# Recurrent stage of a decoder layer: new counted delays, and three groups of matmuls in other places of the order

## The chip, the cores and the metric

The kernel runs on one core of one Trainium2 chip. A core has a matrix engine (PE, whose weight loads are the row PEld), a vector engine (DVE), a scalar engine (ACT), a general engine (POOL) and a queue that issues transfers (SP). They work side by side and wait for each other through semaphores. Each works through its own instructions in the order in which they were issued. The metric is the time of one execution in microseconds (us), as the device measures it.

## The reference, cut to what matters

One layer of a decoder on 1024 tokens of width 1024. The first sub-layer joins a recurrent branch and an attention branch, each weighted by a sigmoid gate; then come a cross-attention into 256 memory tokens and a gated convolutional MLP. The change lies in the recurrent branch (8 heads of 64). What it computes, per token:

```python
w_log = -softplus(-(w0 + tanh(wl) @ w2)) - 0.5
decay = exp(-exp(w_log))
a = sigmoid(a0 + al @ a2)
kk = k * k_k
kk = kk / max(sqrt(sum(kk * kk, axis=-1)), 1e-12)     # per head
k = k * (1.0 + (a - 1.0) * k_a)
erase, refill = -kk, kk * a
def step(state, inp):
    r_t, w_t, k_t, v_t, a_t, b_t = inp
    sa = einsum('bhvk,bhk->bhv', state, a_t)
    state = state * w_t + sa * b_t + v_t * k_t
    return state, einsum('bhvk,bhk->bhv', state, r_t)
_, y = lax.scan(step, state0, (r, decay, k, v, erase, refill))
y = (y - mean(y)) * rsqrt(var(y) + GN_EPS) * gn_g + gn_b
mixed = (g_a * (y_a @ merge_p_a) + g_b * (y_b @ merge_p_b)) @ mix_w_o
```

## The kernel before, in words

Large products are made in float32 as three passes (`mm3`, lines 196 to 198: high times high, high times low, low times high) over 512 columns. Such a group of three matmuls is called a **triple** below.

The recurrent stage works on **8 units**: four head pairs, each in two halves of 512 tokens, each half in 8 chunks of 64 tokens. For every unit there are five generators, each of which issues a few instructions and then yields:

- `operands(i)`: the decay products (`pw`, `pa`, lines 583 and 585), the scan over the logarithms (`CU`), the exponentials; the square of the key (`TMP`, line 601, on ACT) and its sums per head (`vs`, line 549, on PE), the way back (`bc`, line 564), the scaled keys, and the product `gl` (line 632). From `gl` comes the triangular matrix `LT`, of which 16 by 16 blocks go through DRAM (`d1`), are inverted on DVE by substitution (`stmp` and `DB`, lines 654 and 655), and come back through DRAM (`d2`) as `DD` and `EE` (line 667, 16 transfers issued by SP).
- `couplings(i)`: `gb`, `gk`, then three transposes of four blocks each (`tr`, line 707: of `BB`, `KB_` and the values `Xv`), whose results ACT copies out (`KS`, line 721) or DVE copies out after taking the mean away (`ZV` and `SV`, line 719, eight instructions behind one reduction, line 711), and the bonus product `pbo` (line 728), copied out by DVE (`BV`, line 729).
- `inverse(i)`: five small products (`q`, `d`, `e`, `q`, `e`) that finish the inverse from its blocks.
- `recurrence(i)`: for each chunk three products one after another: `x` (line 783), `sa` (788), `z` (794). Each needs what DVE or ACT copied out of the one before.
- `outputs(i)`: `psy`, the group norm (another `vs` and `bc`), the store to `ya`.

The order on PE alone is written out by the program when it is built: a loop keeps a **counted clock**. A generator yields two numbers: how long the work just issued counts on PE, and how long after that its next step comes due. At every turn the loop takes the first class with a due step, in the order of the line below, so that dense work fills what the recurrences leave:

```python
classes = (recurrences, outputs_, inverses, couplings_, operands_, dense, [wide])
```

`dense` are the input projections of this branch (`prj`), `wide` the products of the merge gates (`gt`); each step of both is one triple and counts 0.69. All 256 gate triples are needed later. Those that the recurrent stage did not take are issued between and inside the blocks of the attention stage behind it, by `fill`, at a fixed number per block; after the gates `fill` goes on with the merge products (`mg`), and what is left of those runs in one piece behind the attention blocks. An inverse comes due `L_SUBST = 36` counted us after its `gl`. The other engines' orders come from the scheduler of the language.

PSUM banks go round: the products named `pw`, `pa`, `vs`, `bc`, `gl`, `gb`, `gk`, `tr` and `pbo` take three banks in turn, so that each waits until the result three places ahead of it was copied out.

Of the kernel before, what the change touches and what calls it, by code (L numbers as in the profile page):

```python
# [126 lines left out]
def layer_kernel(ctx: ExitStack, tc, I, out, cst):  # L127
# [42 lines left out]
    def pss(name="pss"):  # L170
        return bank("s", name)
# [322 lines left out]
    def e2(name):  # L494
        return rp.tile([P, HALF], F32, tag="e", name=name, bufs=9)
# [79 lines left out]
    def operands(me):  # L575
# [3 lines left out]
        lo = LO[:, half * HALF:(half + 1) * HALF]  # L579
        cs_ = slice(hp * P, hp * P + P)  # L580

        ps = pss("pw")
        PE.matmul(ps, lw[0:64, cs_], lo[0:64], start=True, stop=True)
        ps2 = pss("pa")
# [7 lines left out]
        S.activation(E2, CU, AF.Exp, scale=DEC)  # L592
        G.tensor_tensor(E3, CU, E3, op=OP.subtract)
        S.activation(E3, E3, AF.Exp, scale=-DEC)
        yield 1.3, 0.5
        while not projections[3 * hp].done:
            yield 0, 0.5
        Xk = Xs[hp, 1][half]

        TMP, KKN = e2("TMP"), e2("KKN")  # L600
        S.activation(TMP, Xk, AF.Square, scale=pc("rwkv_k_k", hp))
        w = norm_sums(TMP, pss, ew, 64.0, None)
        yield 1.0, 4.5
        while not projections[3 * hp + 1].done:
            yield 0, 0.5
        Xr = Xs[hp, 0][half]
# [64 lines left out]
    def couplings(me):  # L671

        u, (hp, half) = units[me], divmod(me, 2)
        Xr, E3, ET, BH, KH, BB, KB_, TMP = u.operands
        Xv = Xs[hp, 2][half]
        AMR = k8("AMR")
        for h, rw in enumerate(rows_h):
            V.tensor_tensor(AMR[rw, :, 1, h, :], r8(Xr[rw]), r8(ET[rw]), op=OP.mult)
            S.activation(AMR[rw, :, 0, h, :], r8(E3[rw]), AF.Copy)

        GB, KS, SV, ZV = k2("GB"), k4("KS"), k4("SV"), k4("ZV")
        u.AMR, u.GB, u.KS, u.SV, u.ZV = AMR, GB, KS, SV, ZV
        if half == 0:
            for h, rw in enumerate(rows_h):
                G.memset(ZV[rw, 0, h, :], 0.0)
        yield 0, 3.0
        ps = pss("gb").rearrange("p (c t) -> p c t", t=CH)
        for c in range(NC8):
            for h, rw in enumerate(rows_h):
                PE.matmul(ps[rw, c], BH[rw, c * CH:(c + 1) * CH], AMR[rw, c, 1, h, :], start=True, stop=True)  # L690
        V.tensor_tensor(GB, ps, bc(gmask[:, CH:P], NC8), op=OP.mult)
        for j in range(2):
            ps = pss("gk").rearrange("p (c a t) -> p c a t", a=2, t=CH)
            for ci in range(4):
                c = 4 * j + ci
                for h, rw in enumerate(rows_h):
                    PE.matmul(ps[rows_h[1 - h], ci], KH[rw, c * CH:(c + 1) * CH], AMR[rw, c, :, h, :], start=True, stop=True)
            for h in range(2):
                rx = rows_h[1 - h]
                m = gmask[rx].rearrange("p (a t) -> p a t", a=2)[:, None].to_broadcast([64, 4, 2, CH])  # L700
                V.tensor_tensor(AMR[rx, 4 * j:4 * j + 4, :, h, :], ps[rx], m, op=OP.mult)
        yield 2.9, 1.0

        for src, flip, dsts in ((BB, 0, (KS,)), (KB_, 1, (KS,)), (Xv, 1, (ZV, SV))):
            ps = pss("tr").rearrange("p (c n) -> p c n", n=P)
            for c in range(4):
                PE.transpose(ps[:, c, :], src[:, c * P:(c + 1) * P], ident)
            if src is Xv:

                mv = sm.tile([P, 4, 2], F32, name="vm", tag="vm", bufs=2)  # L710
                V.tensor_reduce(mv, ps.rearrange("p c (h d) -> p c h d", h=2), axis=AX.X, op=OP.add)
            for q, rq in enumerate(rows_h):
                for h in range(2):
                    ro = rows_h[1 - h] if flip else rows_h[h]
                    for dst in dsts:
                        o, v = dst[ro, q:NC8:2, h, :], ps[rq, :, h * 64:h * 64 + 64]
                        if src is Xv:
                            m = mv[rq, :, h][:, :, None].to_broadcast([64, 4, 64])
                            V.scalar_tensor_tensor(o, m, -1.0 / 64, v, op0=OP.mult, op1=OP.add)
                        else:  # L720
                            S.activation(o, v, AF.Copy)
            yield 0.5, 0.8
        if me >= 2:
            while not outputs_[me - 2].done:
                yield 0, 0.5
        u.BV = ec("BV")
        ps = pss("pbo")
        PE.matmul(ps, ones, TMP, start=True, stop=True)
        V.scalar_tensor_tensor(u.BV, ps, 64.0, Xv, op0=OP.mult, op1=OP.mult)
        yield 1.1, 0  # L730

    def inverse(i):
# [5 lines left out]
            for rw in rows_h:  # L738
                PE.matmul(ps[rw, c, :], UU[rw, c], DD[rw, c], start=True, stop=True)
        S.activation(QQ, ps, AF.Copy)  # L740
        yield 0.8, 1.2
        ps = bank("b", "d1").rearrange("p (c d) -> p c d", d=CH)
        for c in range(NC8):
            for h in range(2):
# [2 lines left out]
        for h in range(2):  # L747
            a = slice(h * 64, h * 64 + 32)
            V.tensor_tensor(DD[a, :, 0:32], DD[a, :, 0:32], ps[a, :, 0:32], op=OP.add)
        yield 0.5, 1.2  # L750
        ps = bank("b", "e1").rearrange("p (c d) -> p c d", d=CH)
        for c in range(NC8):
            for h, rw in enumerate(rows_h):
                PE.matmul(ps[rw, c, :], QQ[rw, c], EE[rw, c, h], start=True, stop=True)
        for h, rw in enumerate(rows_h):
            V.tensor_tensor(EE[rw, :, h], EE[rw, :, h], ps[rw], op=OP.add)
        yield 0.8, 0.8
        ps = bank("b", "q2").rearrange("p (c d) -> p c d", d=CH)
        for c in range(NC8):
            for h in range(2):  # L760
# [2 lines left out]
        for h in range(2):  # L763
            b = slice(h * 64 + 32, h * 64 + 64)
            S.activation(QQ[b, :, 0:32], ps[b, :, 0:32], AF.Copy)
        yield 0.5, 1.0
        ps = bank("b", "e2").rearrange("p (c d) -> p c d", d=CH)
        for c in range(NC8):
            for h in range(2):
# [8 lines left out]
    def recurrence(i):  # L778
        u, (hp, half) = units[i], divmod(i, 2)
        AMR, EE, KS, SV, ZV, WC = u.AMR, u.EE, u.KS, u.SV, u.ZV, u.WC  # L780
        for c in range(NC8):
# [1 line left out]
            PE.matmul(ps[:, 0:P], pair(AMR[:, c, 0]), pair(ZV[:, c]), start=True, stop=True)  # L783
            XS = sm.tile([P, P], F32, name="XS", tag="XS", bufs=2)
            V.tensor_copy(XS, ps[:, 0:P])
            yield 0.3, 1.1
            ps = bank("c", "sa")
            PE.matmul(ps[:, 0:P], pair(EE[:, c]), XS, start=True, stop=True)
            V.tensor_copy(SV[0:64, c, 0, :], ps[0:64, 0:64])
            S.activation(SV[64:128, c, 1, :], ps[64:128, 64:128], AF.Copy)  # L790
            yield 0.3, 1.3
            if not (half == 1 and c == NC8 - 1):
                ps = bank("c", "z")
                PE.matmul(ps[:, 0:P], pair(KS[:, c]), pair(SV[:, c]), start=True, stop=True)
# [2 lines left out]
                for h, rw in enumerate(rows_h):  # L797
                    dst = ZV[rw, c + 1, h, :] if c < NC8 - 1 else units[i + 1].ZV[rw, 0, h, :]
                    V.scalar_tensor_tensor(dst, ZV[rw, c, h, :], WC[rw, c, :], ps[rw, h * 64:h * 64 + 64], op0=OP.mult, op1=OP.add)
                yield 0.3, 1.7  # L800

    def outputs(i):
        u, (hp, half) = units[i], divmod(i, 2)
# [12 lines left out]
        S.activation(Y, psy, AF.Copy)  # L816
        Y2 = ey("Y2")
        S.activation(Y2, Y, AF.Square)
        yield 2.8, 2.5
        w = norm_sums(Y2, pso, ew, 1.0, epsgn)  # L820
        yield 1.0, 4.0
        ps = norm_back(w, pso)
# [45 lines left out]

    def may_project(hp, j):
        if hp == 0:  # L870
            return first.done
        return couplings_[2 * hp - 1].done if j == 2 else couplings_[2 * hp - 2].done and hasattr(units[2 * hp - 1], "WC")

    def gates_timed():
# [2 lines left out]

    first = Task(decays())
    projections = [Task(projected(hp, j), (lambda hp=hp, j=j: may_project(hp, j))) for hp in range(4) for j in (1, 0, 2)]
    operands_ = [Task(operands(i), (lambda i=i: first.done if i == 0 else couplings_[i - 1].done)) for i in range(8)]  # L880
    couplings_ = [Task(couplings(i), (lambda i=i: hasattr(units[i], "WC") and projections[i // 2 * 3 + 2].done and (i < 2 or hasattr(units[i - 2], "out")))) for i in range(8)]
    inverses = [Task(inverse(i), (lambda i=i: clock[0] >= getattr(units[i], "due", 1e9)), True) for i in range(8)]
    recurrences = [Task(recurrence(i), (lambda i=i: inverses[i].done and couplings_[i].done), True) for i in range(8)]
    outputs_ = [Task(outputs(i), (lambda i=i: recurrences[i].done)) for i in range(8)]
    wide = Task(gates_timed())
    dense = (first, *projections)
    classes = (recurrences, outputs_, inverses, couplings_, operands_, dense, [wide])
    with tc.manual_schedule(engines={mybir.EngineType.PE}):
        while not all(t.done for t in outputs_):
# [583 lines left out]
```

## Time and profile before

| | us |
|---|---|
| median of 3 runs | 2306.57 (2303.36 to 2312.32) |
| the profiled execution | 2305.22 |
| its span, first to last instruction | 2303.4 |
| recurrent stage, about | 213 to 790 of the span |
| attention blocks, about | 840 to 1165 of the span |

The profiled execution took 1.8 us more than its span and stands 1.35 us under the median. In the rows below PE's busy time is that of pipelined matmuls whose ends are modelled. An idle time in brackets stands ahead of an instruction and names what ended it. PEclk is the granted clock of TensorE as a share of full speed (1.00 is 2.4 GHz, 0.50 is 1.2 GHz).

### The profile page before, as it was taken

The page shows a single profiled execution, that of the slowest core. Times are in us where ns is not written, and L with a number is a line of the kernel's source. Part 1 is how long each engine was busy: PE and PEld are TensorE (multiplying, and loading weights), DVE is VectorE, ACT ScalarE, POOL GpSimd, SP SyncE. Part 2 cuts the span into 40 slices and gives each one's busy share as a digit, 9 for nine tenths or more (in the row PEclk, how much of TensorE's full clock was granted, in tenths as well). Part 3 has the DMA queues.
Part 4 walks back from the last instruction along what each step waited for, and adds up shares of the span by engine and source line. Part 5 has one row for each costly group of instructions (what it writes and reads, how often), then busy time and mean ns, then how long its engine had stood idle before and what let it go on. Part 6 is the DMA issues. An engine that isn't in the chain of part 4 may idle for free.

```text
span 2303.4 us, 34187 instructions
## 1 busy us (share of the span) xinstructions
PE 2175.1 (94%) x13508; PEld 1788.7 (78%) x13508; DVE 1256.4 (55%) x2495; ACT 897.4 (39%) x1462; POOL 445.9 (19%) x512
## 2 busy tenths in 40 slices
PE   8989989989899879999999999999999999999998
PEld 7988767777678756766669978898888888888886
DVE  4332566666664278788873834456443434444347
ACT  3332343444343356677751433224231313222232
POOL 1212121221220024444440201021010101001013
PEclk9999989999889989999999999999999999999999
DMA  6344111111112412102134321202111111112112
GB/s 206 111 152 141 37 38 41 39 42 45 35 49 66 118 51 78 56 10 60 51 123 152 115 79 55 92 20 64 46 55 37 55 46 46 51 45 69 46 37 83
DMA packets 197933, 158.07 MB, mean 69 GB/s; under 512 B 49301, under 2 KB 173198, under 8 KB 197774
## 3 DMA queue, kind: packets, MB, share of 16 engines
q1 hardware_dynamic: 186062, 139.11, 20.2%
q10 hardware_dynamic: 11136, 14.68, 1.9%
q0 software_dynamic: 576, 2.10, 0.3%
q8 instruction: 107, 1.75, 0.3%
q14 instruction: 52, 0.43, 0.1%
HBM read 125.86 MB, written 29.98 MB: 68 GB/s over the span
## 4 chain that ended last, share of the span: by engine, by line
PE 77%; DVE 10%; DMA 5%; ACT 3%; issue 3%; POOL 1%; SPq 1%; ACTq 0%; DVEq 0%; POOLq 0%
PE up L198 7%; PE up L196 7%; PE up L197 7%; PE dn L196 4%; PE dn L198 4%; PE dn L197 3%; PE op L196 2%; PE op L198 2%; PE op L197 2%; PE gt L196 2%; PE gt L197 2%; PE gt L198 2%; PE prj L196 2%; PE prj L197 2%; DVE wl L202 2%
## 5 line engine op out<-in xcount | busy, mean ns | idle before, releaser
L202 DVE TENSOR_TENSOR wl<-raw,wh 128x1024 fp32r<-128x1024 f32 (+1 forms) x164 | 204.4, 1247 | 274.5 <-ACT wh L201 269.7
L201 ACT ACTIVATE wh<-raw 128x1024 fp32r<-128x1024 f32 (+1 forms) x164 | 173.0, 1055 | 462.8 <-PE dn L198 143.4
L196 PE MATMUL up<-nTh,wh 128*128 128x512 f32 x704 | 276.6, 393 | 0.0
L197 PE MATMUL up<-nTl,wh 128*128 128x512 f32 x704 | 276.5, 393 | 0.0
L198 PE MATMUL up<-nTh,wl 128*128 128x512 f32 x704 | 276.3, 392 | 0.0
L1398 DVE SCALAR_TENSOR_TENSOR cv<-up,pv,cv 128x511 f32<-128x511 f32 (+1 forms) x176 | 131.6, 748 | 146.7 <-ACT cv L1396 144.7
L1422 POOL TENSOR_TENSOR cv<-cv 128x512 f32<-128x512 f32 x44 | 56.7, 1290 | 631.3 <-DVE cl L1402 413.9
L198 PEld LDWEIGHTS up<-nTh,wl 128*128 128x128 f32 x704 | 132.3, 188 | 29.8
L197 PEld LDWEIGHTS up<-nTl,wh 128*128 128x128 f32 x704 | 132.3, 188 | 29.5
L196 PEld LDWEIGHTS up<-nTh,wh 128*128 128x128 f32 x704 | 132.3, 188 | 29.5
L1044 POOL TENSOR_TENSOR pl<-pe,ph 128x512 fp32r<-128x512 f32 x87 | 113.1, 1305 | 161.1 <-ACT ph L1043 134.7
L196 PE MATMUL dn<-wh,gT 128*128 128x512 f32 x352 | 138.3, 393 | 0.0
L198 PE MATMUL dn<-wh,gT 128*128 128x512 f32 x352 | 137.7, 392 | 0.0
L197 PE MATMUL dn<-wl,gT 128*128 128x512 f32 x352 | 137.0, 390 | 0.0
L196 PE MATMUL gt<-xTh,wh 128*128 128x512 f32 x256 | 114.9, 449 | 8.1 <-ACT gst L472 8.1
L1433 DVE SCALAR_TENSOR_TENSOR acc<-acc,dn 128x512 f32<-128x512 f32 x96 | 65.4, 686 | 95.3 <-PE dn L198 94.7
L1396 ACT ACTIVATE cv<-up,pv 128x512 f32<-128x512 f32 x88 | 68.4, 778 | 117.8 <-PE up L198 117.7
L198 PE MATMUL gt<-xTh,wl 128*128 128x512 f32 x256 | 103.2, 403 | 0.0
L197 PE MATMUL gt<-xTl,wh 128*128 128x512 f32 x256 | 103.1, 403 | 0.0
L196 PE MATMUL np<-wh,xTh 128*128 128x256 f32 (+1 forms) x320 | 92.0, 289 | 2.2 <-ACT wh L201 2.2
L196 PE MATMUL prj<-xTh,wh 128*128 128x512 f32 x208 | 91.9, 442 | 1.6 <-ACT wh L201 1.6
L1043 ACT ACTIVATE ph<-pe 128x512 fp32r<-128x512 f32 (+1 forms) x148 | 89.7, 627 | 6.6 <-POOL macc L1161 4.6
(361 smaller groups left out, 5523.8 us busy)
## 6 DMA issues: line engine op xcount, KB each, us to landing
raw<-in_ffn_w_up_dram SPq DMA_DIRECT2D x88, 256.0 KB
raw<-in_w_in_dram SPq DMA_DIRECT2D x37, 512.0 KB
raw<-in_ffn_w_down_dram SPq DMA_DIRECT2D x22, 512.0 KB
gscr<-gst ACTq DMA_DIRECT2D x32, 256.0 KB
xt<-in_x_dram SPq DMA_DIRECT2D x8, 512.0 KB
rawn<-nst SPq DMA_DIRECT2D x32, 128.0 KB
raw<-in_xa_wk_dram SPq DMA_DIRECT2D x8, 512.0 KB
raw<-in_xa_wv_dram SPq DMA_DIRECT2D x8, 512.0 KB
```

The source lines that it names most:

```text
L196: PE.matmul(o, lh, rh, start=start, stop=False)
L197: PE.matmul(o, lh, rl, start=False, stop=False)
L198: PE.matmul(o, ll, rh, start=False, stop=stop)
L201: S.activation(h, src, AF.Copy)
L202: V.tensor_sub(l, src, h.bitcast(F32))
L1043: S.activation(h, e, AF.Copy)
L1044: in_turn("l", LTURN)(l, e, h.bitcast(F32), op=OP.subtract)
L1396: S.activation(c, ps, AF.Identity, scale=pc("cw2", ci), bias=pc("ffn_conv_b", ci))
L1398: V.scalar_tensor_tensor(c[:, s:], ps[:, :HALF - s], pc(nme, ci), c[:, s:], op0=OP.mult, op1=OP.add)
L1422: G.tensor_tensor(c[0], c[0], c[1], op=OP.mult)
L1433: V.scalar_tensor_tensor(v, v, 1.0 if f else ALPHA, ps, op0=OP.mult, op1=OP.add)
```

## The change

It does four things, all in the recurrent stage.

1. In `operands` the square of the key and its sums stand ahead of the decay products, and the first unit's keys are projected ahead of the decay's own inputs (`dense`, `may_project`, `operands_`).
2. In `couplings` the values are transposed first, then `BB` and `KB_`.
3. The counted delays have other values: most in `inverse` are longer, those of `recurrence` are shorter.
4. Nothing is computed otherwise; the number of instructions on PE is the same.

```diff
@@ operands
+        while not projections[3 * hp].done:
+            yield 0, 0.5
+        Xk = Xs[hp, 1][half]
+        TMP, KKN = e2("TMP"), e2("KKN")
+        S.activation(TMP, Xk, AF.Square, scale=pc("rwkv_k_k", hp))
+        yield 0, 1.2
+        w = norm_sums(TMP, pss, ew, 64.0, None)
+        yield 1.0, 0.3
+        while not first.done:
+            yield 0, 0.5
         ps = pss("pw")
         PE.matmul(ps, lw[0:64, cs_], lo[0:64], start=True, stop=True)
...
         S.activation(E3, E3, AF.Exp, scale=-DEC)
-        yield 1.3, 0.5
-        while not projections[3 * hp].done:
-            yield 0, 0.5
-        Xk = Xs[hp, 1][half]
-
-        TMP, KKN = e2("TMP"), e2("KKN")
-        S.activation(TMP, Xk, AF.Square, scale=pc("rwkv_k_k", hp))
-        w = norm_sums(TMP, pss, ew, 64.0, None)
-        yield 1.0, 4.5
+        yield 1.3, 5.0
@@ couplings
-        for src, flip, dsts in ((BB, 0, (KS,)), (KB_, 1, (KS,)), (Xv, 1, (ZV, SV))):
+        for src, flip, dsts in ((Xv, 1, (ZV, SV)), (BB, 0, (KS,)), (KB_, 1, (KS,))):
@@ inverse, behind q, d, e and q
-        yield 0.8, 1.2
+        yield 1.1, 1.2
-        yield 0.5, 1.2
+        yield 0.7, 1.3
-        yield 0.8, 0.8
+        yield 1.1, 1.9
-        yield 0.5, 1.0
+        yield 0.7, 1.1
@@ recurrence, behind x, sa and z
-            yield 0.3, 1.1
+            yield 0.35, 0.8
-            yield 0.3, 1.3
+            yield 0.25, 1.0
-                yield 0.3, 1.7
+                yield 0.25, 1.0
@@ outputs
-        yield 2.8, 2.5
+        yield 2.3, 2.3
@@
-            return first.done
+            return True
...
-    operands_ = [Task(operands(i), (lambda i=i: first.done if i == 0 else couplings_[i - 1].done)) for i in range(8)]
+    operands_ = [Task(operands(i), (lambda i=i: i == 0 or couplings_[i - 1].done)) for i in range(8)]
...
-    dense = (first, *projections)
+    dense = (projections[0], first, *projections[1:])
```

How the instructions of three places stand before and after. First PE, where the last unit's couplings end and its operands begin (`tr<-ident,X` is the transpose of the values, `vs<-csr,TMP` the sums of squares, `x`, `sa`, `z` the recurrence of the unit ahead, `gt` gate triples). Before:

```order
L707 MATMUL tr<-ident,X_6215 128x128 x4
L196 MATMUL gt<-xTh_81,wh 128x512
L197 MATMUL gt<-xTl_83,wh 128x512
L198 MATMUL gt<-xTh_81,wl 128x512
L788 MATMUL sa<-XS,EE 128x128
L728 MATMUL pbo<-TMP_6272,csr 128x512
L583 MATMUL pw<-LO,lw 128x512
L585 MATMUL pa<-LO,lw 128x512
L794 MATMUL z<-SV,KS 128x128
L739 MATMUL q_6757<-DD,UU 64x64 x16
L549 MATMUL vs<-csr,TMP 128x2 x4
L783 MATMUL x<-ZV,AMR 128x128
```

After, the same place (`pbo` stands eight rows ahead of the first row, with `x` and two triples between; the transposes of `BB` and `KB_` lie ahead of that, and the transpose of the values ahead of these):

```order
L790 MATMUL sa<-XS,EE 128x128
L549 MATMUL vs<-csr,TMP 128x2 x4
L796 MATMUL z<-SV,KS 128x128
L196 MATMUL gt<-xTh_85,wh 128x512
L197 MATMUL gt<-xTl_87,wh 128x512
L198 MATMUL gt<-xTh_85,wl 128x512
L593 MATMUL pw<-LO,lw 128x512
L595 MATMUL pa<-LO,lw 128x512
L785 MATMUL x<-ZV,AMR 128x128
```

The sums now come ahead of the decay products, and the bank of `pa` is that of `pbo` where it was that of the transposed values.

Second ACT, the same unit (`E<-pw`, `AG<-pa`, `ET`, `E` are the decay's tanh and exponentials, `TMP` the square). Before:

```order
L586 ACTIVATE E_6739<-pw,hbias 128x512
L588 ACTIVATE AG<-pa,hbias 128x512
L591 ACTIVATE ET<-CU 128x512
L592 ACTIVATE E_6738<-CU 128x512
L740 ACTIVATE UU<-q_6757 128x512
L594 ACTIVATE E_6739<-E_6739 128x512
L601 ACTIVATE TMP<-X_5691,pv 128x512
L553 ACT_TABLE_LOAD
L553 ACTIVATE rs<-rs 128x8
```

After:

```order
L820 ACTIVATE Y_6320<-Y 128x512
L681 ACTIVATE AMR<-E_5916 64x8x64
L586 ACTIVATE TMP<-X_5888,pv 128x512
L555 ACT_TABLE_LOAD
L555 ACTIVATE rs<-vs,epsgn 128x8
```

The square no longer stands behind the tanh and the exponentials of its own unit, but 23 rows ahead of that tanh.

Third PE, one step of the last unit's recurrence, from `z` to the next chunk's `x`. Before:

```order
L794 MATMUL z<-SV,KS 128x128
L196 MATMUL gt<-xTh_82,wh 128x512
L197 MATMUL gt<-xTl_84,wh 128x512
L198 MATMUL gt<-xTh_82,wl 128x512
L196 MATMUL gt<-xTh_82,wh 128x512
L197 MATMUL gt<-xTl_84,wh 128x512
L198 MATMUL gt<-xTh_82,wl 128x512
L196 MATMUL gt<-xTh_82,wh 128x512
L197 MATMUL gt<-xTl_84,wh 128x512
L198 MATMUL gt<-xTh_82,wl 128x512
L783 MATMUL x<-ZV,AMR 128x128
```

After:

```order
L796 MATMUL z<-SV,KS 128x128
L196 MATMUL gt<-xTh_81,wh 128x512
L197 MATMUL gt<-xTl_83,wh 128x512
L198 MATMUL gt<-xTh_81,wl 128x512
L196 MATMUL gt<-xTh_82,wh 128x512
L197 MATMUL gt<-xTl_84,wh 128x512
L198 MATMUL gt<-xTh_82,wl 128x512
L785 MATMUL x<-ZV,AMR 128x128
```

One triple is gone from this step; between `x` and `sa`, and between `sa` and `z`, two triples stand as before. Counted over PE's whole order, 428 triples stand ahead of the last `psy` of the recurrent stage before (208 `prj`, 220 `gt`) and 381 after (208 and 173). Of the 47 gate triples that leave the stage, the attention blocks (from the first `sc` to the last `po`) take in 36.7 more gate and merge triples than before (138.0 for 101.3), the piece behind them 11.3 more merge triples (53.3 for 42.0), and the work between the stages 1 less.

## Rows read from the trace of the kernel before

**Rows 1.** The page: the span, and TensorE's clock in 40 slices.

```profile
span 2303.4 us, 34187 instructions
PEclk9999989999889989999999999999999999999999
```

**Rows 2.** Busy time by stretch: recurrent stage, attention blocks, MLP.

```profile
core 0: us, PE busy (x) PEld busy (x) DVE busy (x) ACT busy (x) POOL busy (x), PEclk, DMA share, GB/s
213.00:790.00 577.00, 525.94 (x4595) 420.10 (x4594) 336.14 (x848) 228.66 (x395) 98.73 (x119) 0.93 0.20 50
840.00:1165.00 325.00, 307.46 (x1476) 210.41 (x1475) 266.17 (x551) 229.25 (x406) 151.48 (x127) 0.98 0.17 49
1900.00:2000.00 100.00, 100.00 (x437) 81.78 (x436) 45.33 (x79) 31.14 (x41) 10.30 (x8) 1.00 0.15 48
```

**Rows 3.** PE's waits, 225 to 790 us (total, times, longest, all us).

```profile
PE vs L549 <- ACT TMP L601: 17.0, 6, 4.7
PE pa L585 <- DVE SV L719: 12.8, 6, 5.7
PE q L762 <- DVE EE L756: 5.4, 7, 1.7
PE pw L583 <- ACT LO L863: 4.1, 1, 4.1
PE z L794 <- ACT SV L790: 2.7, 6, 0.8
PE x L783 <- DVE ZV L799: 0.9, 1, 0.9
```

**Rows 4.** Two of the eight spells at half clock, and all eight summed.

```profile
581.40:595.00 13.60, 10.84 (x55) 7.72 (x56) 3.62 (x9) 5.51 (x9) 2.38 (x4) 0.50 0.08 7
646.30:659.80 13.50, 11.62 (x92) 8.38 (x94) 3.93 (x10) 5.79 (x10) 2.39 (x4) 0.50 0.10 30
...
sum 74.50, PE 58.95 PEld 43.77 DVE 23.49 ACT 30.32 POOL 12.04; mean PE 7.37 PEld 5.47 DVE 2.94 ACT 3.79 POOL 1.51
```

**Rows 5.** Timeline of the last unit's couplings and operands (start, duration).

```profile
641.30 0.60 PE L707 MATMUL tr<-ident,X 128*128 128x128 f32 x4
...
645.66 0.42 DVE L719 SCALAR_TENSOR_TENSOR SV<-vm,tr 64x256 f32<-64x256 f32 x1
...
646.23 2.04 PE L585 MATMUL pa<-LO,lw 64*128 64x512 f32 x2 [0.95 <-DVE SV L719]
...
652.01 0.71 ACT L601 ACTIVATE TMP<-X,pv 128x512 f32<-128x512 f32 x1
...
652.77 1.87 PE L549 MATMUL vs<-csr,TMP 128*128 128x2 f32 x8 [1.88 <-ACT TMP L601]
```

**Rows 6.** Timeline of a recurrence step from z to the next x.

```profile
723.57 0.39 PE L794 MATMUL z<-SV,KS 128*128 128x128 f32 x2
723.99 0.59 DVE L799 SCALAR_TENSOR_TENSOR ZV<-ZV,WC,z 64x64 f32<-64x64 f32 x2 [1.39 <-PE z L794]
725.85 0.39 PE L783 MATMUL x<-ZV,AMR 128*128 128x128 f32 x2
```

**Rows 7.** Timeline of the last unit's way from gl to its inverse.

```profile
670.60 1.15 PE L632 MATMUL gl<-E,BH 64*64 64x64 f32 x32
...
704.75 0.43 SPq L667 DMA_DIRECT2D EE<-d  x1
...
706.07 0.33 PE L739 MATMUL q<-DD,UU 64*64 64x64 f32 x3
```

**Rows 8.** Attention blocks (line 1033, one per block) in two stretches.

```profile
890.00:990.00 100.00, 17.09 (x42) 7.73 (x42) 1.00 0.20 59
1000.00:1070.00 70.00, 16.26 (x36) 6.75 (x36) 0.98 0.09 22
```

**Rows 9.** Merge matmuls (mg) in the same two stretches.

```profile
890.00:990.00 100.00, 39.53 (x136) 24.13 (x134) 7.49 (x11) 1.00 0.20 59
1000.00:1070.00 70.00, 4.00 (x12) 2.19 (x12) 0.00 (x0) 0.98 0.09 22
```

## The prediction

> **What bounds the kernel now.** I read the page first: PE sets the pace nearly everywhere, and the two soft places are the recurrent stage and the attention stage, where the clock row falls under 9 [rows 1]. By stretch, PE is busy for 525.9 of 577 us in the recurrent stage, at a mean clock of 0.93; DVE is at 336 of 577 and ACT at 229, so neither is full. In the MLP PE is busy without a gap, and 437 matmuls in 100 us make 0.229 us for one and **0.686 us for a triple** at full pace [rows 2]. Then the waits of PE: two of them, the sums of squares behind the square (17.0 us) and `pa` behind the copies of the transposed values (12.8 us), are more than half of what PE waits for in the recurrent stage; `q` behind `EE` has 5.4, the first decay product 4.1, `z` 2.7 and `x` 0.9 [rows 3]. The timeline shows why for the last unit. The transposes of the values start at 641.30, and the last of the nine DVE instructions behind them ends at 646.08; `pa` needs that bank and starts at 646.23. The square, which needs only the key, ran on ACT at 652.01, behind the exponentials of the decay, and `vs` waited for it until 652.77 [rows 5]. Just there the clock is at half (1.2 GHz). There are eight such spells, 74.5 us together, PE busy in 59.0 of them [rows 4]. I looked at each: one follows the wait for `LO`, one a wait for the low part of a weight just ahead of a `vs`, and the other six stand on a wait of `vs` or `pa`. So these waits are paid twice, as idle time and as slow matmuls behind it.
>
> All matmuls are still done. Time can only come from waits of PE, from the clock, and from work that now lies in idle time elsewhere.
>
> **The change, part by part.**
>
> *Triples that move.* The order takes 47 gate triples out of the recurrent stage, nearly all from the steps from `z` to `x`: 47 x 0.686 = 32.3 us less there. They come back as 36.7 triples within the attention blocks and 11.3 behind them, less 1 between the stages. Behind the blocks I take them at full price: 7.8 us, and 0.7 off for the one. Within the blocks the price can be read. Where merge triples fill the blocks, 42 blocks took 100 us with 136 / 3 = 45 triples: 2.38 us and 1.08 triples per block; where there was hardly a triple, 36 blocks took 70 us with 4: 1.94 us and 0.11 [rows 8, 9]. So 0.97 triples cost 0.44 us, 0.45 for one: a third of a triple hides behind the softmax. 36.7 x 0.45 = 16.5 us. Net -32.3 + 16.5 + 7.8 - 0.7 = **-8.7 us** (ends: 0 if every triple pays in full, -25 if those in the blocks are free).
>
> *The square and its sums first.* On ACT the square now stands far ahead of its unit's tanh, so `vs` should find it done. Of 17.0 us I leave 2, for the first unit, where only three triples stand between the key's projection and `vs`: **-15** (ends -17 and 0). That they come ahead of `pw` and `pa` costs no work, and the way from `pw` to `gl`, which queues behind them, has counted delays of 5.0, 0.5 and 6.0 to spread over; no wait of `gl` shows before. Projecting the first keys ahead of the decay's inputs leaves the wait for `LO` as it is (4.1).
>
> *The values first.* `pa` now takes the bank of `pbo`, which one DVE instruction empties. It is `pbo` that takes the values' bank. Between those transposes and `pbo` there stand three triples, `x`, `sa`, `z` and two other transposes in four units like the last: 3 x 0.69 + 3 x 0.39 + 2 x 0.60 = 4.4 us [rows 5, 6], where the copies took 4.8. I take 0.5 us for each of eight `pbo`: 4 us in place of 12.8, **-8.8** (ends -12.8, and 0 if DVE is held up by other work).
>
> *Longer delays in the inverse.* The step from `e` to `q` waits 1.9 counted us instead of 0.8 after the same work, one or two triples more. The longest single wait there was 1.7 [rows 3]. I leave 1 of 5.4: **-4.4** (ends -5.4 and 0).
>
> *Shorter delays in the recurrence.* From `z` to `x` the copy into `ZV` ended at 724.58 and `x` started at 725.85: 1.27 us to spare [rows 6], of which a triple less takes 0.69. That holds where DVE is free. `z`, which has had two triples ahead of it all along, waits 2.7 us in sum; I give `x` the same, where it had 0.9: **+1.8** (ends 0, and +40 if every one of some 58 steps stood for the whole triple that left).
>
> *The way through DRAM.* From `gl` to the inverse's first `q` the last unit took 670.60 to 706.07, 35.5 us, with the last transfer issued just 0.9 us before [rows 7]. `L_SUBST` stays at 36 counted us, and until now the waits of `vs` and `pa` often fell into this time and stretched it. Without them `q` comes to stand on the transfers. No row of before has this wait; it is bounded by 0 and by some 5 us per unit, and I take 1.3, what lies here between the start of the last issue (704.75) and `q`: **+10** for eight.
>
> Waits together: -15 - 8.8 - 4.4 + 1.8 + 10 = **-16.4 us**.
>
> *The clock.* At half clock 59.0 us of busy PE hold work that takes half at full clock: 29.5 us are lost [rows 4]. If the waits of `vs` and `pa` go, most of the spells that stand on them should go; the two behind `LO` and the weight stay, and new waits at `q` may make some. I take 18 of 29.5: **-18** (ends -29.5 and 0).
>
> Here a page speaks against the change. The Trainium skill, "TensorE: Matmul & The Clock Gate", section "A second HAM failure mode: psum-queue depth-cycling", says that micro-idles between groups of matmuls can make the clock go back and forth. By that rule a stream with fewer triples between dependent steps would lose clock where this one gains it; no row here shows a spell that began without one of the waits named, so I keep it as a rival below.
>
> **Sum.** -8.7 - 16.4 - 18 = -43 us on the profiled execution's 2305.2: 2262. The median stands 1.35 us above that execution, so **2264 us**.
>
> **Rivals.**
>
> *The waits only move.* PE stands at `q` as long as it stood at `vs` and `pa`, because the way through DRAM and DVE takes its time whatever PE does. For it: the last unit had 0.9 us to spare [rows 7]. Against it: only that unit was so near, and the stage has other waits that still stretch the time. The triples give 8.7, the rest nothing: 2306.6 - 8.7 = 2298. Chance 0.16.
>
> *All of it goes.* No new wait, clock full but for the first spells: waits -30, clock -28, triples -8.7, so 2240. For it: each spell stands on a wait that is taken apart. Against it: DVE and ACT have the same work in less time. Chance 0.08.
>
> *The thinner stream loses clock.* Two triples between steps instead of three, and half clock for twice as long: +29.5 instead of -18, 2306.6 - 8.7 - 16.4 + 29.5 = 2311. For it: the spells lie where small matmuls crowd. Against it: none began away from a wait. This is the page's rule as a mechanism of this kernel. Chance 0.06.
>
> *The substitution comes late (slower).* DVE's share of the stage rises from 336 of 577 to 336 of about 510, the substitution on DVE is pushed back by other work, and every `q` waits for it, with PE's whole queue behind it: recurrence, couplings and gates. At 5.4 us per unit more than I took, the gain of 43 us is gone; at 8 us per unit it is 64 - 43 = 21 us slower: 2328. For it: the margin of the last unit. Against it: the change adds nothing to DVE. Chance 0.08.
>
> **How the numbers follow.** My forecast, 2264 with its own range of 2248 to 2285, has 0.62. A measurement of this kernel tells about 0.5%, 11.5 us, from no change: faster means under 2295, slower over 2318. Faster holds the forecast, the case where all goes, and a third of the case where waits only move (its time lies within a few us of the bound): 0.62 + 0.08 + 0.05 = 0.75. Same holds the rest of that case and most of the thinner stream: 0.16. Slower: the late substitution and a tail of the thinner stream, 0.09. The range of 2243 to 2300 leaves out the two rivals above it (0.14) and the lower half of the case where all goes.
>
> **What would show it.** In the changed kernel's profile: waits of `vs` on `TMP` under 3 us in sum and none of `pa` on `SV`; a few us of `pbo` on `SV`; `q` behind `EE` near 1 us, and a new wait of `q` or `d` on the transfers of `DD` and `EE` of about 10 us; a recurrent stage of some 505 to 520 us instead of 577, with half clock for about 30 us instead of 74.5; attention blocks and the merge behind them together some 24 us longer. The prediction is wrong if the waits at `q` pass 30 us, if half clock stays over 60 us, or if the attention blocks take the added triples at more than their full price.

## The result, and the profile after

The changed kernel takes **2284.07 us** (median of 4 runs, 2277.93 to 2285.88) against 2306.07 beside it on the same chip: a ratio of 0.990, 95% interval 0.987 to 0.992. It is faster, by 22 us where 43 were forecast, and inside the range.

The page of the changed kernel, span and clock [rows 1]:

```profile
span 2282.2 us, 34189 instructions
PEclk9999999999999899999999999999999999999999
```

Busy time by stretch: recurrent stage and attention blocks, each now some 40 us earlier [rows 2].

```profile
213.00:750.00 537.00, 478.44 (x4443) 380.71 (x4442) 332.14 (x844) 218.54 (x383) 99.20 (x119) 0.96 0.19 48
800.00:1147.00 347.00, 331.80 (x1627) 234.83 (x1625) 270.87 (x568) 243.92 (x423) 156.01 (x130) 1.00 0.17 52
```

PE's waits in the recurrent stage, 213 to 742 us (total, times, longest), against [rows 3]:

```profile
PE pbo L730 <- DVE SV L721: 14.6, 5, 5.1
PE prj L198 <- DVE wl L202: 11.3, 4, 9.7
PE z L796 <- ACT SV L792: 7.5, 15, 2.0
PE pw L593 <- ACT LO L865: 4.7, 1, 4.7
PE tr L709 <- DVE SV L721: 3.8, 1, 3.8
PE x L785 <- DVE ZV L801: 3.7, 8, 0.8
PE prj L196 <- ACT wh L201: 2.6, 3, 1.0
PE q L741 <- DMA DD<-d: 2.3, 2, 1.3
...
PE q L764 <- DVE EE L758: 0.3, 1, 0.3
```

The two great waits of before, `vs` behind `TMP` (17.0) and `pa` behind `SV` (12.8), are gone, and `q` behind `EE` with them. In their place stand `pbo` and a transpose behind the same value copies, 18.4 us, and a projection behind `wl` (the low part of a weight, made on DVE), which before was:

```profile
PE prj L198 <- DVE wl L202: 2.8, 2, 2.3
```

In sum PE waits **58.0 us** up to the last `psy` at 742.1; before it was 50.6 up to 782.1. So the waits didn't shrink at all.

The spells at half clock, two of nine and all summed [rows 4]:

```profile
430.60:440.80 10.20, 4.99 (x14) 0.50 0.22 64
...
502.30:509.10 6.80, 4.80 (x10) 0.50 0.43 129
...
sum 44.20, PE 35.23; mean PE 3.91
```

PE is busy for 35.2 us of them, so 17.6 us are lost where it was 29.5 (an estimate, as in the prediction: half of PE's busy time there). The account of the stage, which ends 40.0 us earlier: 47 triples x 0.686 = -32.3, waits +7.4, clock -11.9, together -36.8, 3 us unexplained. From the last `psy` to the first `op` behind the merge (the attention stage) it is 447.8 us instead of 429.4, +18.4. All that follows is unchanged (1092.2 and 1091.9). 40.0 - 18.4 - 0.3 = 21 us, the difference of the spans.

Where the new waits come from is seen on DVE. Timeline of DVE (start, duration) behind the transposes of the values that start at 494.00, with some rows left out:

```profile
495.80 0.32 DVE L656 TENSOR_TENSOR stmp<-DB,LB 64x100 f32<-64x100 f32 x1
496.15 0.69 DVE L713 TENSOR_REDUCE vm<-tr 128x8 f32<-128x512 f32 x1
...
497.23 0.41 DVE L721 SCALAR_TENSOR_TENSOR ZV<-vm,tr 64x256 f32<-64x256 f32 x1
497.67 0.37 DVE L656 TENSOR_TENSOR stmp<-DB,LB 64x121 f32<-64x121 f32 x1
...
502.99 0.42 DVE L721 SCALAR_TENSOR_TENSOR ZV<-vm,tr 64x256 f32<-64x256 f32 x1
503.44 0.35 DVE L657 TENSOR_REDUCE DB<-stmp 64x14 f32<-64x196 f32 x1
503.82 0.42 DVE L721 SCALAR_TENSOR_TENSOR SV<-vm,tr 64x256 f32<-64x256 f32 x1
```

and PE at its longest wait, and at the place just shown:

```profile
435.81 0.80 PE L198 MATMUL prj<-xTh,wl 128*128 128x512 f32 x1 [9.70 <-DVE wl L202]
...
498.72 0.44 PE L796 MATMUL z<-SV,KS 128*128 128x128 f32 x2
504.30 2.08 PE L730 MATMUL pbo<-TMP,csr 128*128 128x512 f32 x2 [5.15 <-DVE SV L721]
```

The value copies stand between instructions of the substitution (`stmp`, `DB`) and of the recurrence, all on DVE. It is the same unit's substitution: its `gl` ran at 474.5, 19.5 us ahead of these transposes, where in the kernel before 33.9 us lay between (484.4 and 518.3, the same unit) and the substitution was done at 505.1. From the start of the transposes to the end of the last copy it takes 494.00 to 504.24, 10.2 us, where it took 4.8 with next to nothing between [rows 5]. PE reaches `pbo` 5.15 us too early and stands idle, with recurrence, gates and projections queued behind it. At 435.81 it is much the same: the weight's `wl` runs at 434.55, behind a unit's value copies (425.90 to 432.49) and its substitution.

### The profile page after: what moved, and what is told of

The parts are those of the page before. It is cut to its first block, busy times and chain, and to the rows that moved or that the text cites. A ratio compares the mean times of both kernels' runs of the same rounds, so it can differ in the third digit from the quotient of the medians.

```text
span 2282.2 us, 34189 instructions
## 1 busy us (share of the span) xinstructions
PE 2150.6 (94%) x13508; PEld 1774.9 (78%) x13508; DVE 1256.9 (55%) x2495; ACT 898.3 (39%) x1459; POOL 451.6 (20%) x512
## 4 chain that ended last, share of the span: by engine, by line
PE 75%; DVE 11%; ACT 4%; DMA 4%; issue 3%; POOL 1%; SPq 1%; ACTq 0%; DVEq 0%; POOLq 0%
PE up L196 7%; PE up L198 7%; PE up L197 7%; PE dn L196 4%; PE dn L198 4%; PE dn L197 4%; PE op L197 2%; PE op L196 2%; PE op L198 2%; DVE wl L202 2%; PE prj L196 2%; PE prj L198 2%; PE prj L197 2%; PE gt L196 2%; PE np L196 1%
## 5 line engine op out<-in xcount | busy, mean ns | idle before, releaser
L196 PEld LDWEIGHTS up<-nTh,wh 128*128 128x128 f32 x704 | 132.3, 188 | 29.5
L198 PE MATMUL prj<-xTh,wl 128*128 128x512 f32 x208 | 83.3, 401 | 11.3 <-DVE wl L202 11.3
```

The source lines that it names most:

```text
L196: PE.matmul(o, lh, rh, start=start, stop=False)
L198: PE.matmul(o, ll, rh, start=False, stop=stop)
```

## The experiments

All ratios are to the kernel before, measured beside each on the same chip. Below, "stage end" is the start of the last `psy`; "waits" PE's waits from 213 us to there; "clock" half of PE's busy time in the half-clock spells there; "attention" from there to the first `op`. These four are from the one profiled execution, triples from the order.

| run | us | ratio (95%) | stage end | triples in stage | waits | clock | attention |
|---|---|---|---|---|---|---|---|
| before | 2306.07 | 1 | 782.1 | 428 | 50.6 | 29.5 | 429.4 |
| after | 2284.07 | 0.990 (0.987 to 0.992) | 742.1 | 381 | 58.0 | 17.6 | 447.8 |
| squares_first | 2273.82 | 0.986 (0.985 to 0.988) | 745.5 | 429 | 32.3 | 15.2 | 431.2 |
| values_first | 2309.66 | 1.001 (1.000 to 1.002) | 781.4 | 428 | 57.5 | 28.7 | 427.6 |
| delays_only | 2340.01 | 1.015 (1.013 to 1.016) | 771.7 | 365 | 70.0 | 40.1 | 470.8 |
| values_last | 2270.53 | 0.984 (0.983 to 0.986) | 728.1 | 381 | 43.3 | 13.3 | 446.3 |
| no_subst | 2254.97 | one execution, no interval | 712.5 | 381 | 41.5 | 6.3 | 447.3 |
| pbo_own_bank | 2280.24 | 0.988 (0.987 to 0.990) | 738.1 | 381 | 53.1 | 15.5 | 448.1 |
| vl_old_rec | 2282.22 | 0.990 (0.988 to 0.991) | 765.4 | 423 | 39.6 | 29.7 | 421.8 |
| vl_old_inv | 2267.69 | 0.983 (0.981 to 0.985) | 737.8 | 382 | 45.9 | 19.5 | 440.6 |
| vl_sv_pool | 2264.82 | 0.981 (0.980 to 0.983) | 724.1 | 381 | 43.1 | 14.5 | 448.1 |
| sv_pool | 2273.97 | 0.985 (0.984 to 0.987) | 731.6 | 381 | 52.0 | 12.8 | 448.0 |
| sf_sv_pool | 2272.68 | 0.985 (0.983 to 0.987) | 741.5 | 429 | 34.4 | 10.0 | 431.1 |
| short_rec_pool | 2263.84 | 0.981 (0.980 to 0.982) | 728.1 | 382 | 44.5 | 15.2 | 441.4 |

### The parts one by one

**squares_first**: before, with the square and its sums ahead, the first diff of `operands`, and nothing else.

> Before, with the first edit alone (the square and its sums ahead of the decay products, the first keys ahead of the decay's inputs). Theory A, that DVE's copies of the transposed values, run in turns with the substitution, make PE wait wherever the bank ring needs them: the waits of vs on TMP (17.0 us before) go, those of pa on SV stay near 12.8 or move to a neighbour of pa in the ring; about 15 us less with some clock, 2290. Theory B, that the new waits come from the shorter delays: the same here, 2285 to 2290. If neither, vs waits for another thing and the time stays over 2300.

**values_first**: before, with only

```
-        for src, flip, dsts in ((BB, 0, (KS,)), (KB_, 1, (KS,)), (Xv, 1, (ZV, SV))):
+        for src, flip, dsts in ((Xv, 1, (ZV, SV)), (BB, 0, (KS,)), (KB_, 1, (KS,))):
```

> Before, with the second edit alone (the values transposed first). Theory A: the wait of pa on SV (12.8 us before) turns into one of pbo on SV of about the same size, 8 to 15 us, and the time stays within 5 us of before, 2301 to 2311. Theory B: with the old delays there is time enough, pbo waits under 4 us, and the time falls by 8 us or more, under 2298.

**delays_only**: before, with only the new numbers in `inverse`, `recurrence` and `outputs`.

> Before, with the third edit alone (the counted delays). The order then has 365 triples in the recurrent stage, 63 fewer. Theory A: the stage gives away 43 us of triples of which the attention stage gives back some 33, but vs and pa still wait, and longer, since fewer triples stand ahead of them: 2290 to 2305. Theory B: the shorter delays make new waits of their own at the recurrence and at the copies, over 15 us in sum: 2305 to 2320.

**values_last**: the whole change without the values first (the diff of values_first, taken back).

> The changed kernel with the second edit taken back (the values transposed last again; the same 381 triples in the stage). Theory A: pbo no longer waits on SV, pw, vs or pa do instead for about as long, 12 to 20 us, and the time is within 4 us of the changed kernel's 2284. Theory B: the values first are worth 8 to 9 us, so this kernel takes 2292 or more.

One part alone gives 32 us, more than the whole change, and its time lies under what either theory allowed. Waits are 18.3 us fewer and 14.3 us less is lost to the clock. PE's waits with the squares first:

```profile
PE q L741 <- DMA DD<-d: 5.5, 3, 2.5
PE z L796 <- ACT SV L792: 5.0, 10, 1.0
...
PE pw L593 <- DVE SV L721: 3.8, 2, 3.6
```

The square's wait is gone, as forecast, and so, which I had not seen, is most of the wait behind the value copies, although the values are still transposed last: `vs` and its delay now stand between `pbo` and the decay products. The bank of the values goes to `pw` instead of `pa`, with more work ahead of it; 12.8 us become 3.8. That is the gain that I had put to the values' new place.

The values first alone hardly change the time (1.001), and on top of the other two parts they cost 13.5 us (2284.07 against 2270.53; 0.990 against 0.984, and the intervals are apart). Neither theory on values_last allowed that. The theory that the new delays caused the new waits, and that the values first were worth 8 or 9 us, falls. So does the other one in so far as it called them worth nothing. In the run with values first alone `pbo` waits seven times, 11.3 us:

```profile
PE vs L549 <- ACT TMP L601: 27.1, 6, 5.2
PE pbo L728 <- DVE SV L719: 11.3, 7, 2.4
```

and `vs` waits 27.1 us where it was 17.0, so that more than the wait of `pa` (12.8) came back in two other places. The delays alone are 33 us slower, beyond both expectations. They take 63 triples (43 us) out of the stage, but it ends only 10 us earlier, because the triples were the cover of the old waits:

```profile
PE pa L585 <- DVE SV L719: 20.2, 6, 5.7
PE vs L549 <- ACT TMP L601: 13.0, 4, 3.8
PE z L794 <- ACT SV L790: 6.9, 12, 1.7
```

Waits and lost clock grow by 19.4 and 10.6 us, and the attention stage by 41.4: its blocks take in 36.7 more triples, as in the change, and the piece behind them the 27.3 that are left over, which is 19.2 us longer. Behind squares first and values last the same delays are worth 3 us (0.986 to 0.984, intervals overlap): what a delay is worth hangs on which waits its triples cover.

### Is it DVE that is late?

**no_subst**: the change, with the substitution cut to its first row.

```
-        for i in range(1, 16):
+        for i in range(1, 2):
```

> The changed kernel without rows 2 to 15 of the substitution on DVE (that part of the inverse is left out). Theory C, that values first is dear because DVE runs the nine copies in turns with the substitution while pbo is only three places behind in the bank ring: pbo's wait on SV falls from 14.6 us to under 6, the 9.7 us of prj behind wl go, and the time is 2255 to 2268. Rival D, that the distance in the ring alone does it, whatever DVE does besides: pbo's wait stays over 9 us and the time over 2270.

**pbo_own_bank**: the change, with `pbo` in a bank of the group norm's, outside the ring.

```
-        ps = pss("pbo")
+        ps = pso("pbo")
```

> The changed kernel with pbo in the outputs' bank, outside the ring, so that vs is now three places behind the transposed values and has x, sa, two triples and its own delay more ahead of it. Rival D: the wait of 14.6 us at pbo falls to under 5 us at vs, and the time to about 2270, that of the kernel with the values last. Theory C: only part of it goes, vs waits 5 to 12 us and the 9.7 us behind wl stay: 2274 to 2282.

Without the substitution on DVE:

```profile
PE z L796 <- ACT SV L792: 10.9, 15, 2.0
...
PE pbo L730 <- DVE SV L721: 5.6, 3, 2.1
...
PE tr L709 <- DVE SV L721: 4.6, 2, 3.8
```

`pbo` falls from 14.6 to 5.6, `wl` from 11.3 to 2.0, and the time to 2254.97, at the lower edge of theory C's range. So the substitution has a large part in DVE's being late; the run also shortens the way to `q` and DVE's load as a whole, so it doesn't price the mixing by itself. But of the 18.4 us behind the value copies 10.2 stay (`pbo` 5.6, `tr` 4.6). The changed kernel's own trace shows the other part. In three of its units no product of the substitution starts between the values' transposes and the last copy, and 8.5 of the 18.4 us stand there (`pbo` 3.00 and 1.70, `tr` 3.78). The third unit, whose transposes start at 377.14, from DVE and PE:

```profile
376.73 1.38 DVE L703 TENSOR_TENSOR AMR<-gk,csr 64x512 f32<-64x512 f32 x2
...
378.73 0.68 DVE L703 TENSOR_TENSOR AMR<-gk,csr 64x512 f32<-64x512 f32 x1
...
380.15 0.68 DVE L713 TENSOR_REDUCE vm<-tr 128x8 f32<-128x512 f32 x1
...
385.03 1.12 PE L730 MATMUL pbo<-TMP,csr 128*128 128x512 f32 x2 [3.00 <-DVE SV L721]
```

With the values first, their transposes come straight behind `gk`, and DVE still has some of the four masks of its results (`AMR`) in front of it, here three, with copies of the recurrence and a product of the group norm. Before, the transposes of `BB` and `KB_` and the triples beside them gave DVE time for these. Over the eight units the reduction starts 2.2 us behind the first transpose, where it was 0.8.

The own bank takes `pbo`'s wait away altogether, and the time hardly moves (2280.24, the intervals overlap):

```profile
PE prj L198 <- DVE wl L202: 11.9, 5, 9.7
PE z L796 <- ACT SV L792: 7.9, 15, 1.9
PE x L785 <- DVE ZV L801: 5.1, 10, 1.2
...
PE gb L692 <- DVE BH L615: 4.1, 2, 2.6
PE vs L549 <- DVE SV L721: 3.7, 2, 2.9
```

All waits together are 53.1 us instead of 58.0: most of the 14.6 stand one step further on, behind DVE again. In its time theory C holds and the rival that the ring alone is the cause (some 2270) falls; in the wait of `vs` it is the other way round, 3.7 us, under the rival's 5 and under theory C's 5 to 12. The bank was where PE noticed that DVE was late.

**sv_pool**: the change, with half of the value copies moved to POOL. **vl_sv_pool**: the same on values_last. **sf_sv_pool**: the same on squares_first.

```
-        for src, flip, dsts in ((Xv, 1, (ZV, SV)), (BB, 0, (KS,)), (KB_, 1, (KS,))):
+        for src, flip, dsts in ((Xv, 1, (ZV,)), (BB, 0, (KS,)), (KB_, 1, (KS,))):
...
+            if src is Xv:
+                for h in range(2):
+                    ro = rows_h[1 - h]
+                    G.tensor_copy(SV[ro, :, h, :], ZV[ro, :, h, :])
```

> The whole change, and with it the half of the value copies that makes SV is moved: POOL copies it from ZV, so DVE has four of the eight copies per unit that stand between the transposed values and the free bank. The text computes the same. Theory C (DVE is late there: substitution and copies share it): the bank comes free after half the copies, pbo behind SV falls from 14.6 us to under 6 us (behind ZV or SV), wl behind DVE from 11.3 to under 6, time 2266 to 2276. Rival D (the three places between the transposed values and pbo are too near in the ring whoever copies): pbo keeps 10 us or more, and z or x wait longer for POOL's copy; time 2279 to 2286.

> The kernel with the values last, and SV copied from ZV by POOL (two instructions), so that DVE has four copies for eight behind each transpose of the values. If DVE's load is what is left (z on SV 11.3 us, pw on SV 4.7, x on ZV 3.9): these fall by half and the time to 2260 to 2267. If POOL's copies take DVE's way or come too late for z: 2270 to 2280.

> Before, with the square and its sums first (part 1 alone), and SV copied from ZV by POOL; all delays old. Theory G (POOL's copy gives what it gave behind the change without values first, 5.7 us, because it is DVE time in the substitution that is freed): 2265 to 2270, pw behind SV gone (it was 3.8 us, and a half-clock spell of 6.8 us stands on it). Rival H (the copy matters only where the delays are short): 2271.5 to 2276.

On the change it gives 10 us (0.990 to 0.985, the intervals just touch): `pbo` is down to 4.8, as expected, `wl` stays near its old size, which was not, and all waits together fall from 58.0 to 52.0 only:

```profile
PE z L800 <- ACT SV L796: 11.3, 18, 2.0
PE prj L198 <- DVE wl L202: 10.3, 5, 6.3
PE pbo L734 <- DVE ZV L721: 4.8, 3, 1.7
```

On values_last it gives 5.7 us (0.984 to 0.981, intervals overlap), within the range of its first expectation but not in its way: `pw` behind `SV` went, `z` behind `SV` rose from 11.3 to 14.5 and `x` stayed. With all delays old it takes `pw`'s wait away and the time stays where it was (0.985 and 0.986, intervals overlap): the rival was right there, `q` waits for DRAM instead, 7.1 us where it was 5.5.

How long the copies take was in the trace of before, had I read all units. From the start of the values' transposes to the end of the last copy, in us, by unit (worked out from the records of these instructions; in brackets how many products of the unit's own substitution start between the reduction and the last copy):

```
before         9.5(4) 7.0(1) 4.8(0) 4.8(0)  5.4(0) 5.9(0) 4.8(0) 5.4(0)  mean 6.0
after          6.8(4) 5.4(0) 7.8(0) 9.6(4) 10.2(4) 7.1(0) 8.9(2) 8.2(0)  mean 8.0
squares_first  9.3(4) 8.9(3) 6.3(0) 5.4(0)  5.4(0) 5.5(0) 6.5(0) 5.5(0)  mean 6.6
values_last    9.1(4) 8.3(1) 5.6(0) 8.1(1)  8.6(2) 9.9(5) 5.9(0) 6.0(0)  mean 7.7
no_subst       4.9(0) 6.8(0) 8.0(0) 7.7(0)  5.2(0) 7.1(0) 5.2(0) 8.7(0)  mean 6.7
sv_pool        4.3(2) 4.4(0) 6.3(0) 6.5(2)  6.8(2) 5.6(0) 7.0(2) 6.8(0)  mean 6.0
```

In values_last the copies take nearly as long as in the change, 7.7 us, and yet PE waits only 4.7 us behind them, since the next user of their bank is `pw`, with `pbo`, `vs` and its delay ahead of it. So, as it seems, late copies cost what they do in the change only together with a next user that comes soon. How the 13.5 us divide between the two, and `wl`, was not separated.

### The delays

**vl_old_rec** and **vl_old_inv**: values_last, with the old delays of the recurrence, and with the old delays of the inverse and the outputs.

```
@@ vl_old_rec                      @@ vl_old_inv
-            yield 0.35, 0.8       -        yield 1.1, 1.9
+            yield 0.3, 1.1        +        yield 0.8, 0.8
...                                ...
```

(One of three numbers on the left, one of five on the right.)

> Squares first and the inverse's and outputs' new delays, the values last, and the recurrence's old delays (423 triples in the stage instead of 381). If the shorter delays of the recurrence pay only by the third of a triple that hides in the attention blocks, less the waits that they add to z, x and sa: within 5 us of the kernel with all but the values first (2270.5). If a shorter stage is worth its 42 triples: 2290 or more.

> The change without the values first, and with the inverse's and the outputs' old delays; the recurrence's new, shorter delays stay. Of the four pairings of old and new delays on squares first and values last, three are timed: both old 2273.8, new inverse with old recurrence 2282.2, both new 2270.5. Theory E (the two edits add up: shorter recurrence delays give 12 us, longer inverse delays cost 8): 2259 to 2266, half clock in the recurrent stage under 35 us. Rival F (the longer inverse delays pay only once the recurrence is short, because short steps bring q to DRAM's return sooner): 2271 to 2280, with q behind EE at 4 us or more and q behind the transfer of DD above 5 us.

With squares_first and values_last these make a square: both old 0.986, recurrence short 0.983, inverse long 0.990, both 0.984. Shorter recurrence delays give 7 to 12 us, longer delays in the inverse and the outputs cost 3 to 8; only the short recurrence behind the long inverse stands clearly apart (0.990 and 0.984), the other intervals touch or overlap. vl_old_rec fell between its two expectations. Its waits are few (39.6) but its clock is as bad as before's:

```profile
325.10:335.30 10.20, 10.20 (x32) 0.50 0.18 52
420.70:427.50 6.80, 5.08 (x14) 0.50 0.29 80
444.50:454.70 10.20, 9.93 (x82) 0.50 0.19 51
```

These three spells, 27.2 of 68 us, stand on projections that wait for parts of a weight (`wh` 7.1 us in sum, `wl` 6.0): why these parts come late here and not in squares_first, which has about as many triples in the stage (429 for 423), stays open. vl_old_inv came out 2 us above the range of adding up, with 47.8 us at half clock instead of under 35; `q` behind `EE` is back at 5.2 us, as its rival said, without that rival's wait for `DD` (1.9). Neither is settled by it.

**short_rec_pool**: squares first, values last, short recurrence delays, all others old, `SV` by POOL.

> Squares first, the recurrence's short delays, all other delays old, values last, and SV copied from ZV by POOL. If the gains add up (short recurrence delays with the old inverse stood at 0.983 of before; POOL's copy gave 5.7 us with all delays new and 1 us with all delays old), the time is 2258 to 2266 and this is the fastest of the versions. If POOL's copy pays only with the longer inverse delays, as the run with all delays old hints (there it took away the wait of pw and left the time where it was), it is 2265 to 2271. With pw behind SV gone (it was 3.4 us) either way, and q behind EE at 4 to 6 us.

2263.84 us, ratio 0.981 (0.980 to 0.982): the fastest, in the range of adding up, though not distinguishable from vl_sv_pool. It beats the changed kernel by 20 us, with the first part of the change, three of its changed delays and the copy on POOL.

## Why the prediction was right, and where it was off

The sign held and the range held; the size was twice too large. That the time fell inside is owed to the width of the range, and to that extent luck: of the forecast's own range, 2248 to 2285, it met the last us, and one of its two large terms, the waits, came out with the other sign. Of the signs that it named, the stage took 537 us (505 to 520 expected) and half clock 44.2 (about 30).

- **The square first: right.** -15 forecast; the wait of 17.0 is gone altogether. squares_first shows it, and gives the wait behind the value copies as well, for a reason that the prediction did not have.
- **The values first: the step that failed.** I put 4 us of `pbo` in place of 12.8 us of `pa`, -8.8. Measured are 14.6 for `pbo` and 3.8 for a transpose, +5.6, and in time +13.5 for the whole part. The room that I reckoned, 4.4 us between the transposes and `pbo`, is not far from the trace's 5.2 (494.00 to `z`'s end at 499.16). The price was wrong: 4.8 us for the copies came from one unit, the seventh ([rows 5] shows its couplings and the operands of the eighth), which is among the three cheapest of the eight, while the first unit of the same trace took 9.5 with four steps of its substitution between. And it was a price from the old order: in the change the copies take 8.0 us in the mean, as their reduction starts 1.3 us later, behind the masks of `gk` and other work, and more of the substitution stands between. I named "0 if DVE is held up by other work" as the end of the range; DVE was held up in most units, and the wait came out 5.6 us beyond that end.
- **The weights: left out.** `prj` behind `wl` grew from 2.8 to 11.3 us. The rival of the late substitution priced DVE only at `q`; it became late at the value copies and at `wl`, and `q` did not wait for it. Without the substitution `wl` is back at 2.0.
- **The recurrence: mis-sized.** `x` from 0.9 to 3.7 (+1.8 was forecast) and `z` from 2.7 to 7.5, where I expected no change. `z` waits for ACT's half of `SV`. In nine of the fifteen waits (3.5 us) that copy had followed DVE's copy of the other half; in the other six (4.0 us) ACT was busy with other work until then.
- **`q` behind `EE`: right,** 5.4 to 0.3 (-4.4 forecast). vl_old_inv brings back 5.2. But the longer delays seem not worth it: in both pairs of runs the kernel with the old numbers is the faster one, by 8 and 3 us, with intervals that touch or overlap.
- **The way through DRAM: too dear.** +10 forecast, 2.3 measured; 5.5 in squares_first and 7.1 in sf_sv_pool, where PE stands less elsewhere (32.3 and 34.4 us of waits). That this is the reason is not shown: values_last has 14.7 us fewer waits than the change and only 2.5 here.
- **Waits together:** -16.4 forecast, +7.4 measured. This is the whole miss, and more than the 21 us by which the sum was off.
- **The clock: right in kind.** -18 forecast, -11.9 measured. Each of the nine spells in the stage has a wait of at least 0.9 us just ahead of it or in it. The Trainium skill, "TensorE: Matmul & The Clock Gate", section "A second HAM failure mode: psum-queue depth-cycling", tells of a clock that goes back and forth on micro-idles between groups of matmuls. This change with its thinner stream lost less clock than before. Between squares_first and values_last only the delays differ, and with 381 triples for 429 the loss is 13.3 us for 15.2; so the rival of the thinner stream finds no support. delays_only, thinner still, lost more (40.1), on spells that stand on waits of 0.97 us and longer. Not every spell has such a wait: one of 3.4 us in values_last (from 583.7) has none longer than 0.56 us in the 8 us ahead of it.
- **The triples: near.** Inside the attention blocks, from the first `sc` to the last `po`, 14.2 us (354.2 before, 368.4 after) for 36.7 triples, 0.39 for one, where 0.45 was forecast; behind them 4.7 against 7.8. A part of it is clock: by the estimate used above 8.7 us were lost in the blocks before and 3.3 are now, and without that a triple would come to 0.53. delays_only, whose blocks lose 9.6, pays 22.8 us for the same 36.7 triples, 0.62 for one.

That the new waits at `pbo` come from DVE's being late rests on no_subst, sv_pool and pbo_own_bank together; the share of the masks of `gk` is read from the trace and was not tested by a run. Why `wl` waits 9.7 us at one place in the change and at most 1.0 us in values_last, with nearly the same work on DVE, was seen only as an order in the timeline and not tested by itself.

## What to carry to other kernels

Price a wait by every instance in the trace, the dearest first: the one that is easy to read is often the one that nothing disturbs. A wait on a PSUM bank need not be about the bank: here the engine that empties it had other work in front, a bank more mostly moved the wait by one step (14.6 us of `pbo` went, and 4 us of time), and taking half of the copies from that engine gave 10. When a product is moved ahead, ask what its copying engine still has to do for the one that is now in front of it. Try a bundle of edits part by part: here one part was worth 32 us, one cost 13, and the new numbers went from +33 to about -3 us (not clear of noise) by what stood beside them.

## What the runs showed of the hardware that was not expected

- What a wait costs in clock does not follow its length. Before, waits of 0.95 and 1.88 us stand at the start and in the middle of 13.5 us at half clock [rows 4, 5]; after, a wait of 9.70 us (to 435.81) runs into 10.2 us of it, in which PE was busy for only 5.0. After, a wait of 0.96 us that ends at 459.72 stands ahead of 3.4 us (from 461.3), and a wait of 1.70 us that ends at 540.22 is followed by none until 618.
- A triple set among the attention blocks cost 0.39 us instead of 0.686 here, 0.53 without the clock's part, and 0.62 in delays_only: between a tenth and two fifths of it is hidden there.
- Half of the value copies on POOL, which starts only when DVE's `ZV` is there, cost little in the recurrence that reads them: with the values last `z` waits 14.5 us instead of 11.3, all waits of PE together 43.1 instead of 43.3.
